# A decoder layer on one core: 512-column projection passes, and attention weights by differences of the values

## The chip, the cores and the metric

One core of one Trainium2 chip runs one launch of the kernel. The metric is the device time of the launch in microseconds. The core has five engines, each with a queue of its own that it works through strictly in order: PE (TensorE, matmuls and transposes, results to PSUM), DVE (VectorE), ACT (ScalarE), POOL (GpSimd) and SP, which issues nearly all DMA transfers. Every time below comes from one profiled execution, unless it is called a median of runs.

## The reference

One layer (`DEPTH = 1`) over 1024 tokens of 1024 channels, all float32:

```python
h = rms_norm(x, norm1_g)
q, k, v, glu_a, glu_b = split(h @ w_in, 5)                 # 512 columns each
q, k = rms_norm per head (8 heads of 64), times q_norm_g, k_norm_g
# attention, strictly causal, no softmax:
#   beta[t,s] = sigmoid(q_t.k_s / 8), s < t
#   A[t,s]    = beta[t,s] * prod_{s<j<t} (1 - beta[t,j])
#   attn_t    = sum_{s<t} A[t,s] v_s
c = glu_a * sigmoid(glu_b)
c = silu(layer_norm(causal_depthwise_conv31(c)))
x = x + concat([attn, c]) @ w_out
h = rms_norm(x, norm2_g)
g, u = split(h @ w_up, 2)                                   # 2816 columns each
x = x + (silu(causal_depthwise_conv3(g)) * u) @ w_down
```

## The kernel before

**Arithmetic.** Each float32 operand of a matmul is split into a high part (`hi`, an ACT cast to float32r) and a low part (`lo`, what is left, a subtraction on DVE or POOL), and a product is three matmuls, hi·hi, hi·lo and lo·hi (`mm3`, L313 to L315).

**Stages.** In the first stage the eight token tiles of x (128 tokens each) are loaded, squared (L419 on ACT), scaled by their norm (`rs` on POOL, L304 and L305; the scaling L423 on DVE), transposed on PE (`hT`, L432) and split (`h_hi` L436, `h_lo` L437). Then come the projections, in this order on PE: v of heads 0 to 3 (`v0`, its second half behind glu 0), the four gated channel blocks `glu` 0 to 3 of the convolution branch, then k, q of heads 0 to 3 and v of heads 4 to 7 (`k0`, `q0`, `v1`), each of these a pass of 256 columns (`project`, 8 tiles x 8 blocks of 128 channels x 3 matmuls of 128x256), and at last q and k of heads 4 to 7 together (`qk`, 512 columns). Weights come in as `raw`, and become `hi` (L459, ACT) and `lo` (L463, DVE or POOL). `normalized` scales q and k by head: a copy from PSUM (L478), then on ACT eight squares (L483) and eight scalings (L488) of 64 columns.

The convolution runs beside the projections: per channel block 31 taps in sequence on DVE (L615 to L627), 16 terms on ACT (L641) added up on POOL (L644), three closing subtractions (L657 to L659). When all four blocks are closed, `conv_norm` does the layer norm: transposes `ln` (L680), statistics on DVE, transposes `lnT` (L706), gate, product and split, and a store to DRAM.

Attention goes by heads and by tiles of 128 queries (`z{head}_{tile}`). For a query tile with w = 128 to 1024 keys: scores z on PE (L1084, L1085), two sigmoids on ACT, of -z into `nb` (`below`, L1094) and of z into `wt` (`above`, L1097), a running product from the diagonal backwards over `nb` on DVE (`scan`, L1113), and `wt` times the product of the keys behind it on POOL (`times`, L1116). The weights are transposed on PE (`wT`, L1137), split into `th` (a copy, L1146 or L1148, on ACT or DVE) and `tl` (DVE, L1153 or L1158), and multiplied with the split values (`po`, L1165). Between these, PE does the rest of `qk` and the convolution's half of the output projection (`op`).

After attention a second plan adds the attention half of the output projection (`opa`), norms the tokens and prepares the feed-forward part; `u` and `dn` (L1764), the feed-forward matmuls, fill the rest.

**What sets the order.** The first two parts are planned: `add(cost, emit, key, after, takes)` enters an operation with its engine and cost in ns (or several engines to choose from), a key (the time it should come at; `T(us)` turns microseconds of the first stage into keys), what it must follow, and the buffers it takes (`plan.token`). `Plan.run` simulates the engines with these costs and emits the operations in the order that comes out; `in_order` then fixes that order on PE, DVE, ACT and POOL. So the costs and keys decide the order on every engine, and what a wait does on the chip is decided there: an engine waits at its next instruction, and all behind it wait too. A buffer is a numbered slot: `nb` (4, also the pads of the convolution), `wt` (5: two raw-weight slots and three convolution outputs `co`), `whl` (8, split weights), `z` (2 PSUM banks), `s` and `o` (3 each).

## Time and profile before

| | |
|---|---|
| median of 3 runs | 1130.48 us (1130.3 to 1130.74) |
| the profiled execution | 1130.67 us, span 1128.9 us |
| busy, share of the span | PE 98%, DVE 79%, ACT 57%, POOL 54% |
| first stage, up to the first `ln` transpose | 203.6 us |
| attention, first score to last `po` | about 238 to 436 us |
| feed-forward | from about 500 us to the end |

A row of the profile names the line, the engine, the operation and its operands (out<-in), how often it came, its busy time, the mean duration of one, and how long the engine had been idle just before, with what ended that. Rows of DMA issues say when a transfer was asked for. The spans of consecutive matmuls overlap: a 128x512 one lasts 0.39 us in the rows, but the next one starts 0.23 us after it. So a busy PE is not yet a PE at its peak, and what one more matmul costs is read from the starts.

### The profile page before, as it was taken

To read this page: it belongs to the slowest core of one execution; us is meant where nothing else is said; L and a number is where in the kernel's file an instruction comes from. 1 tells how busy PE (TensorE), PEld (TensorE's weight loads), DVE (VectorE), ACT (ScalarE), POOL (GpSimd) and SP (SyncE) were. 2 spreads that over 40 slices of the span, in tenths; PEclk is the share of its full clock that TensorE was granted. 3 is DMA by queue.
4 is the path that set the end of the run, shared out by engine and by line. 5 is a ranking of instruction groups with operands and counts; after the bars stand their busy time and mean duration, and the time that the engine had idled before them with its cause. 6 is when DMAs were issued, how large, how long until landed. Compare 5 with 4: busy or idle time off the path is not lost.

```text
span 1128.9 us, 15893 instructions
## 1 busy us (share of the span) xinstructions
PE 1103.1 (98%) x5639; PEld 931.1 (82%) x5639; DVE 889.3 (79%) x1184; ACT 642.7 (57%) x1293; POOL 608.0 (54%) x519
## 2 busy tenths in 40 slices
PE   7999999999899998999999999999999999999998
PEld 6888899878788886878888888888888888888887
DVE  6399967579998987789887776777776678787795
ACT  6256699587877784663343333333343478776660
POOL 5077848387676752656342233233223189888670
PEclk8999999999999999999999999999999999999999
DMA  8021101223833304442232222222222392303404
GB/s 281 22 57 38 57 20 53 74 99 104 248 106 94 103 39 168 157 148 69 96 110 93 75 93 75 93 75 75 94 80 89 112 353 76 129 24 146 150 1 149
DMA packets 108636, 116.48 MB, mean 103 GB/s; under 512 B 20782, under 2 KB 88590, under 8 KB 108558
## 3 DMA queue, kind: packets, MB, share of 16 engines
q1 hardware_dynamic: 108414, 114.95, 30.9%
q8 instruction: 44, 0.72, 0.3%
q10 hardware_dynamic: 144, 0.52, 0.1%
q14 instruction: 34, 0.28, 0.1%
HBM read 82.95 MB, written 28.31 MB: 99 GB/s over the span
## 4 chain that ended last, share of the span: by engine, by line
PE 90%; DVE 4%; ACT 2%; DMA 2%; issue 1%; POOL 1%; SPq 0%; DVEq 0%; ACTq 0%; POOLq 0%
PE dn L1764 19%; PE u_S L314 7%; PE u_S L315 7%; PE u_S L313 7%; PE u L315 5%; PE u L313 5%; PE u L314 5%; PE po L1165 3%; PE wT L1137 2%; PE v L313 1%; PE v L314 1%; PE v L315 1%; PE glu_b L314 1%; PE glu_a L314 1%; PE glu_b L313 1%; PE glu_a L315 1%
## 5 line engine op out<-in xcount | busy, mean ns | idle before, releaser
L1764 PE MATMUL dn<-wd,wd 128*128 128x512 f32 x768 | 181.4, 389 | 0.0
L1764 PEld LDWEIGHTS dn<-wd,wd 128*128 128x128 f32 x768 | 144.2, 188 | 29.9
L314 PE MATMUL u_S<-bT,aS 128*128 128x512 f32 x264 | 102.8, 389 | 0.8 <-DVE bT L1439 0.8
L1767 DVE TENSOR_TENSOR c<-dn,c 128x512 f32<-128x512 f32 x120 | 81.4, 685 | 27.3 <-PE dn L1764 26.7
L315 PE MATMUL u_S<-bT,aS 128*128 128x512 f32 x264 | 102.7, 389 | 0.0
L313 PE MATMUL u_S<-bT,aS 128*128 128x512 f32 x264 | 102.5, 389 | 0.0
L1116 POOL TENSOR_TENSOR wt<-wt,nb 128x128 f32<-128x128 f32 (+3 forms) x64 | 78.0, 1224 | 42.8 <-DVE nb L1113 29.0
L309 ACT CAST aS<-rawu 128x512 fp32r<-128x512 f32 x63 | 38.9, 621 | 97.4 <-PE u_S L315 63.0
L1669 ACT CAST wd<-rawd 128x512 fp32r<-128x512 f32 x128 | 72.6, 618 | 31.3 <-DMA rawd<-in_w_down_dram 7.7
L1113 DVE TENSOR_TENSOR_SCAN nb<-nb,one 128x128 f32<-128x128 f32 (+3 forms) x64 | 84.7, 1340 | 3.1 <-ACT nb L1094 2.8
L1511 POOL TENSOR_TENSOR s<-rawu 128x512 f32<-128x512 f32 x21 | 29.4, 1400 | 103.6 <-DMA rawu<-in_w_up_dram 97.7
L1668 ACT COPY whole<-rawd 128x512 f32<-128x512 f32 x110 | 63.4, 585 | 25.8 <-DVE wd L1670 12.9
L1517 POOL TENSOR_TENSOR rawu<-rawu 128x512 f32<-128x512 f32 x21 | 29.9, 1426 | 80.7 <-DVE a L310 80.7
L1670 DVE TENSOR_TENSOR wd<-whole,wd 128x512 fp32r<-128x512 f32 x90 | 59.8, 683 | 13.0 <-ACT wd L1669 6.9
L1613 DVE SCALAR_TENSOR_TENSOR y<-gv,cols_a,y 128x1023 f32<-128x1023 f32 (+1 forms) x44 | 60.9, 1384 | 10.2 <-ACT y L1611 10.2
L309 ACT CAST a<-rawu 128x512 fp32r<-128x512 f32 x63 | 39.0, 621 | 50.0 <-PE u_S L315 30.2
L315 PE MATMUL u<-b,a 128*128 128x512 f32 x168 | 65.5, 390 | 0.0
L313 PE MATMUL u<-b,a 128*128 128x512 f32 x168 | 65.5, 390 | 0.0
L314 PE MATMUL u<-b,a 128*128 128x512 f32 x168 | 65.4, 389 | 0.0
L314 PEld LDWEIGHTS u_S<-bT,aS 128*128 128x128 f32 x264 | 49.6, 188 | 11.5 <-POOL raws L1476 1.2
L310 DVE TENSOR_TENSOR aS<-rawu,aS 128x512 fp32r<-128x512 f32 x63 | 53.3, 846 | 6.6 <-ACT aS L309 6.0
L313 PEld LDWEIGHTS u_S<-bT,aS 128*128 128x128 f32 x264 | 49.5, 188 | 10.5 <-ACT bT L1438 0.4
(362 smaller groups left out, 3435.2 us busy)
## 6 DMA issues: line engine op xcount, KB each, us to landing
rawu<-in_w_up_dram SPq DMA_DIRECT2D x44, 512.0 KB
act_d<-y SPq DMA_DIRECT2D x22, 512.0 KB
rawd<-act_d SPq DMA_DIRECT2D x22, 512.0 KB
rawd<-in_w_down_dram SPq DMA_DIRECT2D x22, 512.0 KB
rawo<-in_w_out_dram SPq DMA_DIRECT2D x8, 512.0 KB
m<-conv_d SPq DMA_DIRECT2D x16, 256.0 KB
xt<-in_x_dram SPq DMA_DIRECT2D x8, 512.0 KB
x_part<-xt SPq DMA_DIRECT2D x8, 512.0 KB
```

Source lines behind the costliest of these rows:

```text
L309: nc.scalar.copy(hi, src)
L313: nc.tensor.matmul(ps, a_hi, b_hi, start=first, stop=False)
L314: nc.tensor.matmul(ps, a_hi, b_lo, start=False, stop=False)
L315: nc.tensor.matmul(ps, a_lo, b_hi, start=False, stop=last)
L1113: nc.vector.tensor_tensor_scan(rev, rev, ones_of[0][:, :w], 0.0, op0=ALU.mult, op1=ALU.add)
L1116: nc.gpsimd.tensor_tensor(d["wt"][:, :w], d["wt"][:, :w], d["nb"][:, o + 1:S + 1], op=ALU.mult)
L1613: nc.vector.scalar_tensor_tensor(y[:, j:], g[:, :S - j], par("fw", (KF - 1 - j) * NF + f), y[:, j:], op0=ALU.mult, op1=ALU.add)
L1668: nc.scalar.copy(whole, src)
L1669: nc.scalar.copy(t[:, 0], src)
L1670: lo_engine.tensor_tensor(t[:, 1], whole, f32(t[:, 0]), op=ALU.subtract)
L1764: nc.tensor.matmul(ps, a[:, tok], b, start=first and m == 0, stop=last and m == 2, skip_group_check=True)
L1767: nc.vector.tensor_tensor(sums[c][s], ps, sums[c][s], op=ALU.add)
```

## The change

Three things change, with the order that follows from them.

**Projection passes.** `project` now makes 512 columns in a pass: v of all eight heads (`v`, written to the tiles `v0` and `v1`; two token tiles before glu 0, two behind it, four behind glu 1), and q and k of heads 0 to 3 together (`qk0`), before `qk`. The weights of a pass come in four pieces of 2 channel blocks x 512 columns (two DMAs each). The split weights of glu 0 and 1 and of one piece of `qk0` go to the pads and the `co` buffers. q and k of heads 0 to 3 are scaled by `summed` for all eight tiles, as tiles 6 and 7 of `qk` were before: one wide square on ACT, a `tensor_reduce` and a scaling (two of 256 columns) on DVE.

**The first tile.** The key of the first token tiles is earlier (`5 * t - 2` instead of `2 + 2 * t`), so that x's first tile is scaled ahead of the first split of a weight.

**Attention by parts.** With C(s) the running product from s up to the query, A[t,s] = C(s+1) - C(s), so the sum over A times v equals the sum over C(s) - 1 times (v of s-1, minus v of s). The sigmoid of z and the product with it are gone; `less` takes one from the running product, on POOL or ACT; the scan keeps the masked part at one (`max` with a corner of ones instead of `add` with a diagonal). The values are replaced by their differences once (`differences`): a shift by one token is a DMA from SBUF to SBUF, in 112 and 15 rows and one row across the tiles, then a subtraction of 128x1024 on POOL, two for each half of the heads. The weights stay in the buffer of the scan, which is now one of seven (four `nb`, three `co`).

```diff
-AHEAD_Z, AHEAD_SCAN = 1.7, 0.9
+AHEAD_Z, AHEAD_SCAN = 1.4, 0.5
+SUMMED_FIRST = (0, 1, 2, 3, 4, 5, 6, 7)
...
+    corner = const([P, P], BF16, "corner")
+    nc.gpsimd.affine_select(corner, zero_b, pattern=[[1, P]], base=-P, channel_multiplier=1, compare_op=ALU.is_ge, fill=1.0)
...
+    def differences(blk, key, after, tokens):
+        d = {}
+        def shift():
+            v = qkv["v", blk]
...
+            nc.gpsimd.memset(d["s"][0][0:1, 0, :], 0.0)
+            for n in range(2):
+                for r in (slice(0, 112), slice(112, P - 1)):
+                    nc.sync.dma_start(d["s"][n][r.start + 1:r.stop + 1], v[r, 4 * n:4 * n + 4, :])
+                nc.sync.dma_start(d["s"][n][0:1, 1 - n:4, :], v[P - 1:P, 3 * n:3 + 4 * n, :])
+        x = add("SP", 5000, shift, key, after, tokens)
...
+                (nc.gpsimd if eng == "POOL" else nc.vector).tensor_tensor(v, d["s"][n], v, op=ALU.subtract)
+            subs.append(add({"POOL": 2560}, sub, key, [x]))
...
+    def project(name, parts, ws, t, at_, room):
+        o, d, m = plan.token("o"), {}, None
+        tok = slice((t % 4) * P, (t % 4 + 1) * P)
+        for k in range(ND):
+            def products(k=k):
+                if k == 0:
+                    d["ps"] = bank(o, [P, 512], f"{name}{t}")
+                    room()
+                hi, lo = [ws[k // 2][part].rearrange("p k b c -> p k (b c)") for part in ("hi", "lo")]
+                mm3(d["ps"], h_hi[t // 4][:, k, tok], h_lo[t // 4][:, k, tok], hi[:, k % 2, :], lo[:, k % 2, :], k == 0, k == ND - 1)
...
-        norm_in(t, xl[t], (2 + 2 * t) if t < 4 else (8 + 3 * t))
-    project("v", 0, v0, (0, 1), (12, 18))
+        norm_in(t, xl[t], (5 * t - 2) if t < 4 else (8 + 3 * t))
...
-    for part, blk, at_, pairs in (("k", 0, 124, (0, 1, 2, 3)), ("q", 0, 147, (0, 1, 2, 3)), ("v", 1, 170, (2, 3, 0, 1))):
-        project(part, blk, project_weights(part, blk, at_), pairs, [at_ + 5.8 * i for i in range(4)])
+    done["q", 0] = done["k", 0] = [project("qk0_", (("q", 0), ("k", 0)), w_first, t, FIRST_QK + 5.5 * t, qk_room) for t in range(NT)]
...
-                    def above(d=d, n=n, cs=cs, ce=ce):
-                        nc.scalar.activation(d["wt"][:, cs:ce], d["z", n][:, :ce - cs], AF.Sigmoid)
...
-                    nc.vector.tensor_tensor_scan(rev, rev, ones_of[0][:, :w], 0.0, op0=ALU.mult, op1=ALU.add)
-
-                def times(d=d, o=o, w=w):
-                    nc.gpsimd.tensor_tensor(d["wt"][:, :w], d["wt"][:, :w], d["nb"][:, o + 1:S + 1], op=ALU.mult)
+                    nc.vector.tensor_tensor_scan(rev, rev, ones_of[0][:, :w], 0.0, op0=ALU.mult, op1=ALU.max)
+
+                def less(eng, d=d, o=o):
+                    nb = d["nb"][:, o:S]
+                    if eng == "POOL":
+                        nc.gpsimd.tensor_scalar(nb, nb, 1.0, -1.0, op0=ALU.mult, op1=ALU.add)
+                    else:
+                        nc.scalar.activation(nb, nb, AF.Identity, bias=minus_one)
...
-                b = add("POOL", 310 + 1.5 * w, times, i - AHEAD_SCAN + 0.3 * u, [a] + twos)
+                b = add({"POOL": 100 + 1.03 * w, "ACT": 160 + 0.86 * w}, less, i - AHEAD_SCAN + 0.3 * u, [a])
```

The order on the engines is built from both kernels. On DVE, at the very start (x_q0 and x_k0 hold the first two tiles of x, raw/hi/lo_v are the first weights), the rows are before:

```order
L463 TENSOR_TENSOR lo_v0_0_211<-raw_v0_0_194,hi_v0_0_210 128x1024
L423 SCALAR_TENSOR_TENSOR x_q0_133<-x_q0_133,rs0_207,attn_110 128x1024
L463 TENSOR_TENSOR lo_v0_1_218<-raw_v0_1_196,hi_v0_1_217 128x1024
L423 SCALAR_TENSOR_TENSOR x_q0_133<-x_q0_133,rs1_225,attn_110 128x1024
L437 TENSOR_TENSOR h_lo0_170<-hT0_0_227,h_hi0_169 128x4x128
L437 TENSOR_TENSOR h_lo0_170<-hT0_1_249,h_hi0_169 128x4x128
```

and after the change:

```order
L435 SCALAR_TENSOR_TENSOR x_k0_138<-x_k0_138,rs0_217,attn_110 128x1024
L483 TENSOR_TENSOR lo_v_0_223<-raw_v_0_200,hi_v_0_222 128x1024
L483 TENSOR_TENSOR lo_v_1_228<-raw_v_1_203,hi_v_1_227 128x1024
L449 TENSOR_TENSOR h_lo0_176<-hT0_0_231,h_hi0_175 128x4x128
L449 TENSOR_TENSOR h_lo0_176<-hT0_1_240,h_hi0_175 128x4x128
L435 SCALAR_TENSOR_TENSOR x_k0_138<-x_k0_138,rs1_238,attn_110 128x1024
L483 TENSOR_TENSOR lo_v_2_254<-raw_v_2_207,hi_v_2_253 128x1024
```

The scaling of the first tile has moved ahead of the first weight, and the second tile behind the split of the first.

On DVE, at the end of the last convolution block (conv_a3 and conv_b3 are its two sums), the rows are before:

```order
L627 SCALAR_TENSOR_TENSOR conv_b3_1776<-cpad3_916,cols_b_125,conv_b3_1776 128x512 x7
L527 COPY v1_1880<-v1_2_1881 128x512
L627 SCALAR_TENSOR_TENSOR conv_b3_1776<-cpad3_916,cols_b_125,conv_b3_1776 128x512
L527 COPY v1_1880<-v1_3_1959 128x512
L463 TENSOR_TENSOR lo_qk_0_2104<-raw_qk_0_1877,hi_qk_0_2103 128x1024
L463 TENSOR_TENSOR lo_qk_1_2120<-raw_qk_1_1895,hi_qk_1_2119 128x1024
L657 TENSOR_TENSOR attn_110<-attn_110,conv_a3_1601 128x512
```

and after:

```order
L704 SCALAR_TENSOR_TENSOR conv_b3_1570<-cpad3_1128,cols_b_129,conv_b3_1570 128x512 x2
L577 TENSOR_REDUCE sq_qk0_5_1646<-squares_qk0_5_1648 128x8
L704 SCALAR_TENSOR_TENSOR conv_b3_1570<-cpad3_1128,cols_b_129,conv_b3_1570 128x512 x4
L573 TENSOR_TENSOR q0_1343<-q0_1343,rs_qk0_5_1647 128x256
L573 TENSOR_TENSOR k0_1344<-k0_1344,rs_qk0_5_1647 128x256
L734 TENSOR_TENSOR attn_110<-attn_110,conv_a3_1416 128x512
L577 TENSOR_REDUCE sq_qk0_6_1692<-squares_qk0_6_1694 128x8
```

The reductions and scalings of `qk0` (tiles 0 to 6) now stand between the taps of the last block; `rs_qk0` in them is made on POOL, between the convolution's additions there.

On ACT, in attention, at head 3's query tile 6 (896 keys, two PSUM banks z), before:

```order
L1094 ACTIVATE nb0_0_2591<-z3_6_0_3611 128x512
L1097 ACTIVATE wt3_6_3617<-z3_6_0_3611 128x512
L1094 ACTIVATE nb0_0_2591<-z3_6_1_3614 128x384
L1097 ACTIVATE wt3_6_3617<-z3_6_1_3614 128x384
L1193 COPY attn_110<-po3_0_3571 64x512
```

and after, to the row that takes one from the running product of the same tile:

```order
L1176 ACTIVATE nb1_1_2396<-z3_6_0_3098 128x512
L1176 ACTIVATE nb1_1_2396<-z3_6_1_3102 128x384
L1197 ACTIVATE nb3_5_3085<-nb3_5_3085,minus_one_131 128x768
L1346 COPY prod1_1_3134<-op1_1_3036 128x512
L1226 CAST diagonal_0_1722<-wT3_0_0_3130 128x384
L1228 CAST rest_2108<-wT3_1_0_3136 128x512
L1176 ACTIVATE nb3_7_3152<-z3_7_0_3112 128x512
L1197 ACTIVATE nb1_1_2396<-nb1_1_2396,minus_one_131 128x896
```

The second sigmoid of each bank has gone; 30 of the 64 `less` stand on ACT, 34 on POOL, and 14 copies L1015, L1146 and L1148 have moved from DVE to ACT (29 on DVE before, 15 now).

More of the change, by code (lines that the diff above doesn't have):

```diff
@@ L443, with in_pad, in_co, weights @@
     norm_done = []
-    def weights(name, srcs, shape, at_, key=None):
+    def in_pad(r, shape, name):
+        return cp.tile([P, KC - 1 + S], F32R, tag=f"pad{r.index}", name=name)[:, :S].rearrange("p (k c) -> p k c", k=shape[0]) if len(shape) == 2 else (
+            cp.tile([P, KC - 1 + S], F32R, tag=f"pad{r.index}", name=name)[:, :S].rearrange("p (k b c) -> p k b c", k=shape[0], b=shape[1]))
+    def in_co(r, shape, name):
+        return wide(r, [P] + shape, name, F32R)
+    def weights(name, srcs, shape, at_, key=None, homes=None):
         d, room = {}, plan.token("wt")
-        room.only = (2, 3) if name.startswith("glu") and key is not None else (0, 1)
-        d["rooms"] = [plan.token("whl") for _ in range(2)]
+        room.only = (2, 3) if name in ("v_2", "v_3") else (0, 1)
+        homes = homes or [(plan.token("whl"), lambda r, shape, name: whl([P] + shape, F32R, name, r.index)) for _ in range(2)]
+        d["rooms"] = [r for r, _ in homes]
         def load():
@@ L457, in high @@
         def high():
-            d["hi"], d["lo"] = [whl([P] + shape, F32R, f"{part}_{name}", r.index) for part, r in zip(("hi", "lo"), d["rooms"])]
+            d["hi"], d["lo"] = [home(r, shape, f"{part}_{name}") for part, (r, home) in zip(("hi", "lo"), homes)]
             nc.scalar.copy(d["hi"], d["raw"])
@@ new lines, in summed, with groups, square, scale @@
+    def summed(name, d, o, m, to, at_):
+        room, r, key = plan.token("squares"), plan.token("rs8"), T(at_)
+        def groups(of):
+            return of.rearrange("p (h d) -> p h d", d=DH)
+        def square():
+            d["sq"], d["rs"] = [small.tile([P, 8], F32, tag=f"{tag}8_{r.index}", name=f"{tag}_{name}") for tag in ("sq", "rs")]
+            d["squares"] = squares(room, f"squares_{name}")
+            for n, piece in enumerate(to()):
+                nc.scalar.activation(part_of(d["squares"], n, 512 // len(to())), piece, AF.Square)
+        def scale():
+            for n, piece in enumerate(to()):
+                g = 8 // len(to())
+                nc.vector.tensor_tensor(groups(piece), groups(piece), d["rs"][:, n * g:(n + 1) * g].unsqueeze(2).to_broadcast([P, g, DH]), op=ALU.mult)
+        m = add({"ACT": 600, "DVE": 690}, lambda eng: copy_out(eng, to(), d["ps"]), key, [m])
+        a = add("ACT", 620, square, key, [m], [room, r])
+        b = add("DVE", 690, lambda: nc.vector.tensor_reduce(d["sq"], groups(d["squares"]), axis=AX.X, op=ALU.add), key, [a])
+        c = add("POOL", 1900, lambda: rstd(d["rs"], d["sq"], 1.0 / DH), key, [b])
+        e = add("DVE", 750, scale, key, [c])
+        room.users += [b]
+        r.users += [e]
+        o.users += [m]
+        return e
@@ new lines, in project, with to @@
+    def project(name, parts, ws, t, at_, room):
[8 more added lines that the diff above has]
+                mm3(d["ps"], h_hi[t // 4][:, k, tok], h_lo[t // 4][:, k, tok], hi[:, k % 2, :], lo[:, k % 2, :], k == 0, k == ND - 1)
+            m = add("PE", 685, products, T(at_ + 0.7 * k), [ws[k // 2]["ready"], h_ready[t][k // 4]] + ([m] if m else [] if name == "v" else list(norm_done)), [] if m else [o])
+            for r in ws[k // 2]["rooms"]:
+                r.users += [m]
+        if t > 3:
+            second_used.append(m)
+        def to():
+            return [qkv[part][:, t, :] for part in parts]
+        if name != "v":
+            return (summed if t in SUMMED_FIRST else normalized)(f"{name}{t}", d, o, m, to, at_ + 6)
+        a = add({"ACT": 700, "DVE": 800}, lambda eng: copy_out(eng, to(), d["ps"]), T(at_ + 6), [m])
+        o.users += [a]
+        return a
@@ L843, in to @@
             return qkv["both"][:, t, :]
[L845 to L866 removed]
+        qk_done[t] = (summed if t in SUMMED else normalized)(f"qk{t}", d, o, m, lambda: [to()], at_ + 6)
     for t in range(4, NT):
@@ L871 @@
         conv_norm(n, LN_AT + 10 * n)
+    rooms = [plan.token("wt", free=True) for _ in range(2)]
+    for n, r in enumerate(rooms):
+        r.only = (n,)
+    differences(1, DIFF_AT, done["v", 1] + second_used, rooms)
     def make_one():
@@ L934 @@
         queries_keys(t)
-    early, late = {}, {}
+    early, late, n_tile = {}, {}, [0]
     base = 0.0
```

167 lines of the change are left out of this document (79 added, 88 removed).

## The prediction

> **What bounds the kernel now.** I read the page's shares and chain first, then the stages, then the waits of the stage in which PE stands.
>
> ```profile
> span 1128.9 us, 15893 instructions
> PE 1103.1 (98%) x5639; PEld 931.1 (82%) x5639; DVE 889.3 (79%) x1184; ACT 642.7 (57%) x1293; POOL 608.0 (54%) x519
> PE 90%; DVE 4%; ACT 2%; DMA 2%; issue 1%; POOL 1%; SPq 0%; DVEq 0%; ACTq 0%; POOLq 0%
> ```
>
> The profiled execution took 1130.67 us, 1.8 outside its span and 0.2 over the median. PE carries the chain. By stages (first column of each engine: busy us):
>
> ```profile
> 0.00:20.00 20.00, 13.73 (x60) 9.18 (x61) 10.89 (x14) 13.12 (x21) 9.23 (x17) 0.83 0.95 320
> 20.00:203.00 183.00, 183.00 (x1183) 167.49 (x1183) 141.08 (x187) 117.14 (x317) 110.65 (x95) 1.00 0.18 53
> 203.00:238.00 35.00, 34.91 (x190) 28.84 (x188) 22.11 (x37) 23.18 (x71) 19.54 (x29) 1.00 0.18 66
> 238.00:436.00 198.00, 187.56 (x1183) 161.76 (x1182) 182.34 (x225) 156.08 (x333) 137.11 (x123) 0.99 0.38 114
> 436.00:520.00 84.00, 78.91 (x364) 63.05 (x363) 66.80 (x96) 45.12 (x87) 45.73 (x47) 0.98 0.45 150
> ```
>
> From 20 to 238 us PE never rests: there time is only had by giving PE less to do. In attention (238 to 436) PE is idle for 10.4 us, and DVE is busy for 182.3 of 198. So the start, the passes and attention are three different questions.
>
> **1. Passes of 512 columns.** PE loses 768 matmuls of 256 columns (v, k and q: 2 x 2 x 8 tiles x 8 blocks x 3) and gets 384 of 512. Their starts:
>
> ```profile
> 19.24 0.28 PE L314 MATMUL v<-lo_v,h_hi 128*128 128x256 f32 x1
> ...
> 20.20 0.28 PE L313 MATMUL v<-hi_v,h_hi 128*128 128x256 f32 x1
> ...
> 99.81 0.39 PE L313 MATMUL glu_b<-h_hi,hi_glu_b 128*128 128x512 f32 x1
> ...
> 100.72 0.39 PE L314 MATMUL glu_b<-h_lo,hi_glu_b 128*128 128x512 f32 x1
> ```
>
> Eight starts of 256 columns take 0.96 us, 0.120 each; four of 512 take 0.91, 0.2275 each. 768 x 0.120 - 384 x 0.2275 = 92.2 - 87.4 = 4.8 us less, all of it where PE never rests. By rounding of the starts (0.01 us) the bounds are 3.5 to 6. [...]
>
> The wider passes need 24 loads of 256 KB on SP instead of 8 of 512 and 8 of 256 KB; in 20 to 203 the transfers fill 18% of the queues, and that covers them. If it were gone, a late piece would stop PE at its first matmul: the split weights of v stay in all eight `whl` slots until v's last tile, so those of glu 2 are made only behind the last use of a piece, with 18 matmuls (4.1 us) of cover for a cast (1.04 us, below) and a split (1.22). glu 3's load waits on SP behind the shift of the values, that is for v's last tile, and has the 21.8 us of glu 2 (96 x 0.2275) as cover. I take 0, at worst 1 us.
>
> **2. The start.**
>
> ```profile
> 7.71 0.56 POOL L305 TENSOR_TENSOR rs<-rs,expo 128x1 f32<-128x1 f32 x1
> 7.80 1.04 ACT L459 CAST hi_v<-raw_v 128x1024 fp32r<-128x1024 f32 x1 [0.46 <-DMA raw_v<-in_w_in_dram]
> 8.88 1.23 DVE L463 TENSOR_TENSOR lo_v<-raw_v,hi_v 128x1024 fp32r<-128x1024 f32 x1 [7.20 <-ACT hi_v L459]
> 10.02 1.28 DVE L423 SCALAR_TENSOR_TENSOR x_q<-x_q,rs,attn 128x1024 f32<-128x1024 f32 x1
> 10.57 1.06 ACT L419 ACTIVATE attn_first<-x_q 128x1024 f32<-128x1024 f32 x1 [0.23 <-DMA x_q<-in_x_dram]
> 11.36 1.97 PE L432 MATMUL hT<-ident_r,x_q 128*128 128x128 f32 x8 [3.39 <-DVE x_q L423]
> 14.60 1.94 PE L432 MATMUL hT<-ident_r,x_q 128*128 128x128 f32 x8 [1.27 <-DVE x_q L423]
> 16.55 0.41 PE L314 MATMUL v<-lo_v,h_hi 128*128 128x256 f32 x1
> 16.76 0.41 PE L315 MATMUL v<-hi_v,h_lo 128*128 128x256 f32 x1
> ```
>
> `rs` is there at 8.27, the scaling waits behind `lo_v` until 10.02. Put first, it runs 8.3 to 9.6, and `hT` 9.6 to 11.6. The first `h_hi` on ACT follows the square of the second tile (10.57 to 11.8, its load still the fourth of SP): 12.4. So v begins at 12.4, where before PE ran without a break from 14.6: 2.2 us. Against it, the cast, scaling and split of pieces 3 and 4 run between, about 1.2 us each on DVE; by 17.4 all four are split, and PE then still has half of the first v tile. At the start the clock is half (starts 0.21 us apart at 256 columns, 0.120 at 19.24), and if it rises at the same moment as before, only 0.8 of the 2.2 is left. I take 1.8, bounds 0.5 and 2.6. Ten transfers (v's other half among them) now stand before glu 0's; PE has 11 us of v for them, 16 x 0.5 MB at the 320 GB/s of the first row end by 27 us and glu 0 starts at about 29: cover enough, just.
>
> **3. The last convolution block.**
>
> ```profile
> L617 DVE SCALAR_TENSOR_TENSOR conv_a<-cpad,cols_b,conv_a 128x512 f32<-128x512 f32 x60 | 45.3, 755 | 2.0
> L659 DVE TENSOR_TENSOR conv_out<-attn,conv_b x4: 672/678/680, 86.8 to 198.5; 128x512 f32<-128x512 f32 x4
> L680 PE MATMUL ln<-ident_r,conv_out x32: 270/272/273, 203.6 to 231.0; 128*128 128x128 f32 x32
> L862 DVE TENSOR_TENSOR qk<-qk,rs_qk x2: 1007/1258/1508, 239.6 to 256.0; 128x512 f32<-128x512 f32 x2
> L920 DVE TENSOR_TENSOR qk<-qk,rs_qk x8: 399/415/415, 235.4 to 290.8; 128x256 f32<-128x256 f32 x8
> L860 DVE TENSOR_REDUCE sq_qk<-squares 128x8 f32<-128x512 f32 x1 | 0.7, 678 | 0.0
> ```
>
> Before, block 3 closes at 199.2 and `ln` starts at 203.6: 4.4 us to spare. After, PE ends glu 3 at about 151 (13.3 us of start, then 7 of `hT`, 43.7 of v, 87.4 of glu) and `qk0` at 195; three `ln` follow at once, in front of `qk`. DVE ends block 2 at about 157 (it starts at 130 behind glu 2), and block 3 then takes 31 taps (0.675 from start to start), three closings (0.6), six reductions (0.6) and twelve scalings (0.34 each, the 415 of L920 less the same 0.08): 30.3 us, 187. The scalings wait for `rs` on POOL, behind the convolution's additions there, some 0.4 us each time: 190. With both operands in SBUF they may also wait for POOL itself: L862 took 1007 and 1508, where twice L920 (which reads PSUM) is 830. Six tiles x 0.2 to 0.7 are 1 to 4 us: 191 to 194, just in time. PE stands 0 to 5 us; I take 1. [...]
>
> **4. Attention.**
>
> ```profile
> L1113 DVE TENSOR_TENSOR_SCAN nb<-nb,one 128x128 f32<-128x128 f32 (+3 forms) x64 | 84.7, 1340 | 3.1 <-ACT nb L1094 2.8
> L1116 POOL TENSOR_TENSOR wt<-wt,nb 128x128 f32<-128x128 f32 (+3 forms) x64 | 78.0, 1224 | 42.8 <-DVE nb L1113 29.0 <-PE qk L314 4.0 <-PE z L1085 2.5
> L1097 ACT ACTIVATE wt<-z 128x512 f32<-128x512 f32 (+2 forms) x96 | 47.9, 501 | 0.3
> L1148 DVE CAST rest<-wT 128x512 fp32r<-128x512 f32 x9 | 6.1, 681 | 0.4 <-PE po L1165 0.4
> L1146 DVE CAST diagonal<-wT 128x384 fp32r<-128x384 f32 x13 | 7.0, 540 | 0.9 <-PE wT L1137 0.8
> L1015 DVE CAST keys<-kT 128x512 fp32r<-128x512 f32 x7 | 4.7, 681 | 0.4 <-PE kT L1011 0.4
> L994 POOL TENSOR_SCALAR rest<-v x6: 621/628/630, 255.0 to 392.2; 128x512 fp32r<-128x512 f32 x6
> L1222 ACT CAST w_hh<-rawo 128x1024 fp32r<-128x1024 f32 x4 | 4.1, 1072 | 0.0
> DVE tl L1158 <- ACT rest L1148: 4.1, 7, 1.0
> DVE nb L1113 <- ACT nb L1094: 2.8, 6, 0.8
> DVE diagonal L1153 <- ACT diagonal L1146: 1.7, 2, 1.6
> DVE rest L1052 <- ACT keys L1049: 1.4, 2, 1.2
> DVE attn L1196 <- ACT attn L1193: 1.0, 3, 0.4
> ```
>
> DVE is the engine nearest its end, and 11.0 of its 15.7 idle us are waits for ACT (the last five rows). ACT loses 47.9 and gets 30 `less` (650 keys on average; between 0.7, a copy's rate by L1222, and 0.9 with its added column) = 21 to 27, and 14 copies = 7.8: 156 becomes 137 to 143. POOL loses 78.0 and gets 34 `less` (512 keys on average, the same operation as L994, 0.63) = 21 and two subtractions of 2.0: 137 becomes 84. DVE loses 3 x 0.68 + 6 x 0.54 + 5 x 0.68 = 8.7; rows overlap by 0.08, and one split of the convolution comes over from POOL: 6.5 net. The scan with `max` I take as the scan with `add`; no row shows another. One chain gets shorter too, since a large tile waits 2.0 us for `times` now and 1.1 for `less`, and its two z banks for one sigmoid each instead of two.
>
> So DVE's 182.3 become 176, and of its idle 15.7 I take a quarter off, as ACT's load falls by a tenth and the rest are chains: 176 + 12 = 188, 10 us less. Bounds: the whole idle gone would be 22 us, but PE's own starts (288 x 0.11, 320 x 0.12, 192 of z, 192 + 68 x 0.2275 and 124 x 0.11) fill 175 of the 198 already, so 20; at the other end, work off DVE gains nothing if the chains hold, and 30 new waits of ACT for a scan cost: a loss of 6. The shift of the values (1 MB per half of the heads) and its subtractions lie 100 us before their use: 0.
>
> **5. Behind attention** the order is the same, but the last split of w_out stands before the last sum of attention instead of behind it: 0.5 us less, bounds 0 and 1.2.
>
> **Sum:** 1130.7 - 4.8 - 1.8 + 1 - 10 - 0.5 = 1114.6, and by the median's 0.2, 1114.4.
>
> **The rivals.** (a) Attention is held by its chains: the order on every engine is fixed by costs in ns, and PE and DVE already alternate. For it: DVE's second cause of idleness is its own late work. Attention gains 4 and the whole ends at 1120.4. [...] (c) Slower: the 30 `less` on ACT wait for a scan, up to 2.27 us long, and behind them on ACT stand sigmoids and copies on which PE and DVE wait. Before, nothing on ACT waited for DVE's scan. The forecast's 16 us are eaten when each costs 0.54 us on the path; at 0.7 the time is 1135. Against it: `less` stands behind other rows in ACT's order, which cover a scan. (d) Everything in attention falls to PE's own 175 plus 5: 1106.5. (e) The pass saves no time because the weight load bounds it: 1119; the 0.120 and 0.2275 speak against it.
>
> **Chances.** Forecast (1109 to 1118) 0.6, (a) 0.17, (b) 0.08, (c) 0.05, (d) 0.06, (e) 0.04. 1106 to 1122 leaves out (c), part of (a) and of (d). 0.2% is what a measurement of this kernel tells from no change; faster has all cases but (c) and a remainder: 0.93, same 0.02, slower 0.05.
>
> **What the profile after would show.** Right: v's first matmul by 12.4; no idle PE between 20 and 195; `ln` at 195 to 197; the first z at 231 to 234, the last `po` at 420 to 424; DVE's waits for ACT under 8 us. Wrong: PE idle before `ln` with block 3 as releaser; ACT rows released by the scan, with PE waiting for them.

## The result, and the profile after

The changed kernel takes 1132.91 us (median of 12 runs, 1132.33 to 1136.43) against 1130.07 for the kernel before on the same chip (12 runs): the ratio is 1.0028, with a 95% interval of 1.0019 to 1.0037. It is slower by 2.8 us, where 1114.4 was forecast. The profiled execution took 1132.88 us, with this page:

```profile
span 1130.7 us, 14860 instructions
PE 1102.3 (97%) x5255; PEld 909.7 (80%) x5255; DVE 901.8 (80%) x1197; ACT 606.9 (54%) x1083; POOL 552.1 (49%) x487
```

ACT and POOL have 36 and 56 us less to do, PE has 384 matmuls less, and yet PE is busy for as long as before (1103.1) and the span is longer by 1.8. To see where, both spans are cut at the same events: the end of the projections of the first heads (the first `qk` of heads 4 to 7 before, the first `ln` after), the first `z`, the first product with w_out that belongs to attention (`opa`), the first `u` of the feed-forward part, and its first `dn`. The stages of before, then of after (columns: the stretch, its length, busy us of PE, PEld, DVE, ACT, POOL with instructions, the granted clock, share and GB/s of DMA):

```profile
0.00:201.56 201.56, 195.29 (x1234) 175.49 (x1235) 150.90 (x200) 129.51 (x336) 119.88 (x111) 0.98 0.26 79
201.56:238.23 36.67, 36.58 (x197) 30.22 (x196) 23.18 (x38) 24.16 (x74) 19.77 (x29) 1.00 0.18 66
238.23:436.31 198.08, 187.64 (x1184) 161.75 (x1182) 182.65 (x225) 156.10 (x333) 136.88 (x123) 0.99 0.38 115
436.31:493.38 57.07, 53.07 (x249) 42.67 (x248) 41.61 (x67) 30.79 (x62) 28.84 (x34) 0.97 0.51 179
493.38:915.38 422.00, 420.91 (x1856) 347.69 (x1857) 320.99 (x389) 166.82 (x244) 147.85 (x104) 1.00 0.30 97
```

```profile
0.00:197.69 197.69, 192.56 (x851) 155.16 (x852) 161.81 (x209) 97.87 (x167) 107.55 (x103) 0.98 0.26 79
197.69:243.66 45.97, 39.19 (x205) 32.35 (x203) 32.15 (x57) 29.46 (x84) 27.90 (x37) 0.93 0.33 105
243.66:437.15 193.49, 183.00 (x1178) 158.55 (x1175) 176.21 (x215) 147.60 (x279) 85.43 (x91) 1.00 0.39 121
437.15:490.38 53.23, 51.29 (x250) 41.47 (x248) 39.70 (x64) 29.92 (x61) 28.54 (x34) 1.00 0.52 178
490.38:917.30 426.92, 426.59 (x1857) 348.95 (x1858) 322.94 (x389) 166.42 (x244) 148.32 (x104) 1.00 0.29 96
```

Row by row: -3.9, +9.3, -4.6, -3.8 and +4.9, +1.9 together; behind `dn` it is -0.1, which makes the 1.8 by which the spans differ. Two rows eat what the other three gain, and each is a story of its own.

**The second row** holds the waits of PE that were forecast as 1 us. The timeline of PE, its waits, and DVE's last subtraction of a convolution block (L736) and its scalings (L573, with least, median and greatest ns):

```profile
197.69 0.49 PE L757 MATMUL ln<-ident_r,conv_out 128*128 128x128 f32 x3
204.59 2.15 PE L757 MATMUL ln<-ident_r,conv_out 128*128 128x128 f32 x9 [6.42 <-ACT q L528]
206.40 0.78 PE L325 MATMUL qk<-hi_qk,h_hi 128*128 128x512 f32 x1
L736 DVE TENSOR_TENSOR conv_out<-attn,conv_b x4: 677/678/679, 84.6 to 203.8; 128x512 f32<-128x512 f32 x4
L573 DVE TENSOR_TENSOR q<-q,rs_qk x8: 417/481/1306, 164.3 to 211.5; 128x256 f32<-128x256 f32 x8
L573 DVE TENSOR_TENSOR k<-k,rs_qk x8: 418/1412/2622, 165.5 to 211.9; 128x256 f32<-128x256 f32 x8
```

PE turns three of the four conv blocks of the first `ln` and stops at the fourth. The row names ACT's copy; what also had to be there is block 3, and its last subtraction started at 203.8 and took 0.68 us, up to 0.1 us before PE goes on. The matmul behind then takes 0.78 us in place of 0.39: the granted clock was 0.74 in the pause (197.8 to 204.5) and 0.51 from 204.6 to 207.9 (0.93 over the second row). Of the 9.3 us, 6.7 are PE's idle time (45.97 less 39.19, where it was 0.1), 0.9 are eight more transposes in the row, and the other 1.7 are slower starts, nearly all of them right behind the pause.

**The fifth row** is code that the change does not touch, with the same matmuls, and PE does not wait for more in it (idle for 0.3 us, 1.1 before). PE simply runs slower there, in `u` almost alone. The first and last `u` of one block of 36 and the first `u_S` behind it, after:

```profile
625.80 0.39 PE L325 MATMUL u<-bT,a 128*128 128x512 f32 x1
...
633.93 0.39 PE L327 MATMUL u<-b,a 128*128 128x512 f32 x1
634.16 0.39 PE L325 MATMUL u_S<-bT,aS 128*128 128x512 f32 x1
```

8.36 us for 36 matmuls, 0.2322 each, where before each took 0.2267 (8.16). The `u_S` between take 10.89 per 48, as before.

### The profile page after: what moved, and what is told of

The parts are those of the page before. It is cut to its first block, busy times and chain, and to the rows that moved or that the text cites. A ratio compares the mean times of both kernels' runs of the same rounds, so it can differ in the third digit from the quotient of the medians.

```text
span 1130.7 us, 14860 instructions
## 1 busy us (share of the span) xinstructions
PE 1102.3 (97%) x5255; PEld 909.7 (80%) x5255; DVE 901.8 (80%) x1197; ACT 606.9 (54%) x1083; POOL 552.1 (49%) x487
## 4 chain that ended last, share of the span: by engine, by line
PE 78%; DVE 11%; POOL 3%; ACT 3%; DMA 2%; issue 1%; SPq 0%; POOLq 0%; DVEq 0%; ACTq 0%
PE dn L1844 19%; PE u_S L326 7%; PE u_S L327 7%; PE u_S L325 7%; PE u L326 6%; PE u L325 5%; PE u L327 5%; PE po L1245 2%; POOL attn L721 2%; DVE conv_a L694 2%; PE wT L1217 2%; DVE nb L1190 2%; DVE conv_b L704 1%; PE opa L325 1%; PE opa L326 1%
## 5 line engine op out<-in xcount | busy, mean ns | idle before, releaser
L1190 DVE TENSOR_TENSOR_SCAN nb<-nb,one 128x128 f32<-128x128 f32 (+4 forms) x64 | 84.7, 1341 | 1.6 <-ACT nb L1176 1.4
L322 DVE TENSOR_TENSOR a<-rawu,a 128x512 fp32r<-128x512 f32 x63 | 50.2, 797 | 16.1 <-ACT a L321 16.1
L1593 POOL TENSOR_TENSOR rawu<-s,rawu 128x512 f32<-128x512 f32 x21 | 32.2, 1536 | 53.0 <-DVE a L322 52.2
```

Of the source, the lines that this page charges most:

```text
L322: lo_engine.tensor_tensor(lo, src, f32(hi), op=ALU.subtract)
L1190: nc.vector.tensor_tensor_scan(rev, rev, ones_of[0][:, :w], 0.0, op0=ALU.mult, op1=ALU.max)
```

## Experiments on the unchanged code: where the weights lie

All tiles have the same shape, and the order is the same; what differs is where they lie. The new constants (`corner`, `minus_one` and the longer set of small tiles) move everything allocated behind them in the left pools by 416 bytes. Both kernels also allocate a constant `pad` of 32 bytes that nothing reads, which makes the left pools easy to move.

```diff
 after_moved32, before_moved32:
-    const([P, 8], F32, "pad")
 after_moved96:
-    const([P, 8], F32, "pad")
+    const([P, 32], F32, "pad")
 before_right32:
+    ctx.enter_context(tc.tile_pool(name="edge", bufs=1, side="right")).tile([P, 8], F32, ...)
```

> The changed kernel with the unused 32-byte constant `pad` left out, and nothing else: the order on every engine is the same, but the left pools of SBUF (mixp and what lies behind it) move down by 32 bytes, so that their tiles start at odd multiples of 32 bytes, as in the kernel before, and no longer at multiples of 64. Theory A (the address of the weight tile sets PE's pitch): in the trace of the changed kernel matmuls of 512 columns whose weights start at a multiple of 64 bytes take 233.3 ns from start to start, all others 226.67; here all take 226.67, 36 `u` take 8.16 us in place of 8.36, the stretch from the first `u` to the first `dn` falls from 426.9 to 422, glu 0 and glu 1 fall by 1 us, and the whole by 5 to 6 us: about 1127. Rival B (the unchanged part is slower because other work or code loading falls on it at another moment): the same 426.9, the whole within 1 us of 1132.9.

> The kernel before with the same unused 32-byte constant left out, and nothing else: its left pools move down by 32 bytes, from odd multiples of 32 to multiples of 64. Theory A: the weights `a` of `u`, which lie there, now cost 233.3 ns per matmul in place of 226.67; the stretch from the first `u` to the first `dn` grows from 422.0 by 4 to 5 us, and the whole to 1134.5 to 1136. Rival B: no change, 1130.1 within 1.

> The changed kernel with the unused constant `pad` 128 bytes long in place of 32, same order on every engine: the left pools move up by 96 bytes. The runs so far leave of theory A this form: a matmul of 512 columns takes 226.67 ns where its weights and its moving operand start at the same place modulo 512 bytes, and 232 to 234 where they do not. (Before: all at 480 modulo 512. Changed kernel: weights `a` of `u` at 384. The two kernels moved by 32 bytes have them at 352 and 448: both slow, though 352 and 480 agree modulo 128.) Here `a` is at 480 again: 36 `u` take 8.16 us in place of 8.36, the stretch from the first `u` to the first `dn` about 422 in place of 426.9, and the whole 4 to 5 us less than the changed kernel: 1128 to 1129. Rival B (the place does not matter; something else in the new order slows `u`): 426.9 again, 1132.9.

> The kernel before with 32 unused bytes at the far end of SBUF, so that the right pools (the activations `b` and `bT`, the weights `aS`, `wd`) move down by 32 bytes to 448 modulo 512, while the left pools (weights `a`) stay at 480. Theory A, relative form (weights against moving operand): `u` with `a` on the left against `b` on the right is slow, 8.35 us per 36, while `u_S` and `dn`, with both on the right, stay at 226.67 ns: the whole 4 to 6 us over the kernel before. Rival A2 (absolute form: whatever starts elsewhere than at 480 is slow): `u_S` and `dn`, over 2000 matmuls, are slow as well, 10 to 20 us over. Rival B: no change.

The stretch from the first `u` to the first `dn`, in the order after_moved32, before_moved32, before_right32, after_moved96:

```profile
491.94:918.01 426.07, 425.75 (x1856) 349.32 (x1857) 321.07 (x389) 166.33 (x244) 147.81 (x103) 1.00 0.29 96
491.76:917.16 425.40, 424.31 (x1857) 347.43 (x1857) 321.46 (x389) 166.87 (x244) 148.66 (x104) 1.00 0.30 96
491.39:916.94 425.55, 424.47 (x1856) 347.69 (x1857) 321.74 (x389) 166.67 (x244) 147.66 (x104) 1.00 0.30 96
489.37:911.73 422.36, 421.94 (x1856) 348.79 (x1857) 321.56 (x389) 166.17 (x244) 147.02 (x103) 1.00 0.29 97
```

With the byte at which the tiles start, as the compiled program has it (the first of the three `a` in the left pools, which serve two thirds of `u`; the other two lie multiples of 4096 further), and the ratio of times to the kernel before:

```
kernel           a on the left mod 512  b, bT, aS mod 512   u to dn   ratio [95%]
before           56800        480       480                 422.00    1
changed          57216        384       480                 426.92    1.0028 [1.0019, 1.0037]
after_moved32    57184        352       480                 426.07    1.0015 [1.0005, 1.0026]
before_moved32   56768        448       480                 425.40    1.0038 [1.0025, 1.0051]
before_right32   56800        480       448                 425.55    1.0028 [1.0017, 1.0039]
after_moved96    57312        480       480                 422.36    0.9984 [0.9975, 0.9994]
```

My first form of the theory (a multiple of 64 bytes is slow) fell with after_moved32: 352 is an odd multiple of 32, like 480, and was slow. The form that these rows allow is relative: a 512-column matmul runs at 226.7 ns when its 128x128 weights and its moving operand start at the same place modulo 512 bytes, and at 232.9 to 233.2 on average when they do not (the 540 starts of `u` per kernel with `a` on the left). before_right32 shows that it is relative and not one good address: there `b`, `bT` and `aS` all moved to 448, and `u_S` (both on the right) kept its 10.89 us per 48, while `u` (`a` on the left still at 480) rose to 8.32 per 36.

In the changed kernel the weights of glu 0 and 1, in the convolution's padded tiles (4216 bytes long, so that the next one starts elsewhere) and in `conv_out`'s, show the same: 5.55 to 5.60 us per 24 where 5.44 was seen before. They also show that 512 is too strict, though the expectations above and below are worded with it. The tile `hi_glu_a` of glu 0 starts at 224 modulo 512 in the changed kernel and in after_moved96 alike, against activations at 480; the tile `lo_glu_a`, whose matmuls stand between, starts at 384 in the first and at 480 in the second. The first, then the second:

```profile
41.01 0.39 PE L325 MATMUL glu_a<-h_hi,hi_glu_a 128*128 128x512 f32 x1
...
43.80 0.40 PE L325 MATMUL glu_b<-h_hi,hi_glu_b 128*128 128x512 f32 x1
...
49.37 0.39 PE L325 MATMUL glu_a<-h_hi,hi_glu_a 128*128 128x512 f32 x1
...
52.09 0.39 PE L325 MATMUL glu_a<-h_hi,hi_glu_a 128*128 128x512 f32 x1
```

Twelve starts lie between the two rows of each kernel, and take 2.79 us in the first and 2.72 in the second; those of `hi_glu_a` alone average 233 and 227 ns. So 224 against 480, 256 bytes apart, is fast when its neighbours are, and slow beside a slow one. What the rows bear out is a step of 256 bytes: distances of 0 and 256 were fast; 32, 128, 384, 416 and 480 were slow. Other distances do not occur in these kernels, and why the distance matters no run shows.

No wait of PE is recorded for this (in the fifth row it is idle for 0.3 us), but the same matmuls take nearly 3% longer (233 ns for 226.7) when the two operands lie badly to each other.

## Experiments on the last convolution block

Theory: DVE's scalings, new before 200 us, are drawn out by POOL's additions, as the forecast allowed for in its third part, and close block 3 late. DVE's and POOL's rows at one of them show what is meant:

```profile
185.56 1.09 POOL L721 TENSOR_TENSOR attn<-attn,attn_first 128x512 f32<-128x512 f32 x1
186.38 0.54 DVE L573 TENSOR_TENSOR q<-q,rs_qk 128x256 f32<-128x256 f32 x1
186.72 1.36 POOL L721 TENSOR_TENSOR attn<-attn 128x512 f32<-128x512 f32 x1
186.85 1.52 DVE L573 TENSOR_TENSOR k<-k,rs_qk 128x256 f32<-128x256 f32 x1
...
193.45 2.59 POOL L483 TENSOR_TENSOR lo_qk<-raw_qk,hi_qk 128x1024 fp32r<-128x1024 f32 x1
193.70 2.62 DVE L573 TENSOR_TENSOR k<-k,rs_qk 128x256 f32<-128x256 f32 x1
```

Of the twelve scalings that start before 204, nine are drawn out, and each of them ends 0.27 to 0.29 us behind an instruction of POOL: eight behind an addition, and the longest behind the split of a weight. Alone a scaling takes 0.42.

**Read from PSUM.** The copy out of PSUM goes, square and scaling read the bank:

```diff
-            for n, piece in enumerate(to()):
-                nc.scalar.activation(part_of(d["squares"], ...), piece, AF.Square)
+            nc.scalar.activation(d["squares"], d["ps"], AF.Square)
...
-                nc.vector.tensor_tensor(groups(piece), groups(piece), d["rs"]...)
+                nc.vector.tensor_tensor(groups(piece), groups(part_of(d["ps"], n, 512 // len(to()))), d["rs"]...)
...
-        m = add({"ACT": 600, "DVE": 690}, lambda eng: copy_out(eng, to(), d["ps"]), key, [m])
...
-        o.users += [m]
+        o.users += [a, e]
```

> The changed kernel with the norms of the first heads' queries and keys (and of two tiles of the others) read from PSUM: ACT no longer copies the product out, its square and DVE's scaling read the bank, and the scaling writes the tile in SBUF. In the changed kernel's trace the 16 scalings of 256 columns, whose two operands lie in SBUF, take 418 ns where POOL runs no two-operand addition and 1.2 to 2.6 us where it does, each ending 0.2 to 0.3 us behind POOL's. Theory E (two operands from SBUF wait for POOL; one does not): all take about 0.4 us, DVE has 8 to 9 us less to do before 195, `ln` waits under 1 us, and the whole falls by 6 to 8 us, to 1125 to 1127. Rival F (the scalings were slow for another reason, the broadcast operand): they stay at 0.7 to 1.5 us, and the whole stays within 2 us of 1132.9.

```profile
L572 DVE TENSOR_TENSOR q<-qk,rs_qk x8: 415/417/419, 164.1 to 203.1; 128x256 f32<-128x256 f32 x8
L572 DVE TENSOR_TENSOR k<-qk,rs_qk x8: 411/414/415, 164.4 to 203.4; 128x256 f32<-128x256 f32 x8
```

Measured: 1129.27 us, ratio 0.9991 [0.9982, 0.9999]. All sixteen scalings take 0.41 to 0.42 us, though POOL's additions run beside ten of them; theory E holds, and with it the wait at `ln` is gone (0.4 us is left). The time fell by 3.6 us only (the expectation was 6 to 8), and not where it was looked for: from the first `ln` to z it still takes 46.3 us (46.0 after the change), and attention is 3.6 shorter. The order was worked out anew, more work now stands ahead of z, and PE waits further on:

```profile
PE lnT L781 <- DVE attn L763: 3.7, 2, 2.9
```

**Four scalings by a factor per partition,** in the same order:

```diff
-                nc.vector.tensor_tensor(groups(piece), groups(piece), d["rs"]... , op=ALU.mult)
+                for i, group in enumerate(...):
+                    nc.vector.tensor_scalar(group, group, d["rs"][:, n * g + i:n * g + i + 1], None, op0=ALU.mult)
```

> The changed kernel with each scaling of 256 columns (two operands from SBUF, one of them the factors, broadcast) written as four scalings of 64 columns by a per-partition factor, which leaves one operand in SBUF; the order on every engine is otherwise the same. Theory E (two operands from SBUF wait for POOL's two-operand addition): no scaling is drawn out to the end of an addition; each group of four takes 0.5 to 0.8 us whatever POOL does, against a mean of 0.75 (`q`) and 1.48 (`k`) in 150 to 205; DVE has 3 to 7 us less, PE's wait at `ln` of 6.4 us falls to 0 to 3, the whole by 3 to 7 us: 1126 to 1130. Rival F (the third block is late for its taps and reductions alone): the wait stays at 6.

```profile
L574 DVE TENSOR_SCALAR q<-q,rs_qk x28: 241/249/2333, 164.7 to 213.0; 128x64 f32<-128x64 f32 x28
L574 DVE TENSOR_SCALAR k<-k,rs_qk x28: 239/244/1093, 167.2 to 213.7; 128x64 f32<-128x64 f32 x28
PE ln L758 <- ACT squares_qk L568: 13.0, 1, 13.0
```

1141.2 us, ratio 1.0095 [1.0082, 1.0108]: a miss. A single scaling takes 0.24 us when nothing holds it, but 13 of 40 are drawn out, to the end of POOL's instruction: up to 1.3 us by an addition, and to 2.3 by the split of a weight. So it is not the second operand from SBUF alone: DVE's `tensor_scalar` from SBUF to SBUF waits as well, while the taps (L694, one operand in SBUF, the sum in PSUM) take 756 ns beside the same additions. Why it waits no run here shows.

**`ln` later in the order** (key 199 in place of 190, 33 `qk` ahead of it), and **the norms on ACT** as before the change:

```diff
 after_ln199:
-LN_AT = 190.0
+LN_AT = 199.0
 after_norm_on_act:
-SUMMED_FIRST = (0, 1, 2, 3, 4, 5, 6, 7)
+SUMMED_FIRST = ()
```

> The changed kernel with the key of the convolution's norm at 199 in place of 190: on PE 33 matmuls of `qk` (7.5 us) now stand ahead of the first `ln`, which is where the changed kernel's PE stood for 6.4 us and then ran 2.3 us longer at half clock. Theory C (`ln` was put ahead of work that was ready, and the late third block of the convolution stops PE): no wait at `ln` over 1 us, clock full throughout, z begins at about 237 in place of 243.7, and the whole falls by 5 to 8 us, to 1125 to 1128. Rival D (attention's first tiles are held by DVE, which is late for the same reason): z comes earlier, but PE stands as long between z and the first sums, and the whole stays within 2 us of 1132.9.

> The changed kernel with the norms of the first queries and keys done on ACT as before the change (eight squares with accumulation and eight scalings of 64 columns per tile; the order is worked out anew). DVE loses eight reductions (0.68 each) and sixteen scalings (mean 0.94 in 150 to 230), about 20 us up to the last; ACT gets 64 squares (0.255 and 0.187 for the accumulator) and 64 scalings (0.334) for 16 squares: 43 us more, where it is busy for 23 of 45 us between 150 and 195. Theory K (DVE's new work before 200 made the third block late): `ln` waits under 1 us, and PE reaches the `qk` behind it 7 us earlier. Rival L (ACT then holds PE's banks or the weights' casts): PE waits for ACT between 155 and 200, and the whole is 1130 or more.

```profile
PE qk L325 <- ACT hi_qk L479: 3.7, 1, 3.7
ACT hi_qk L479 <- DMA raw_qk<-in_w_in_dram: 4.6, 1, 4.6
```

after_ln199 took 1142.61 us, ratio 1.0105 [1.0092, 1.0118]. `ln` waits no more, but the `qk` put ahead of it was not ready: its weights come late (the rows above, of that run), and z begins at 247.0. So `ln` did not stand in front of ready work, as theory C had it; two things were late at once. The later z is 3.4 us of the loss, and attention behind it, in another order, is 7.0 us longer. after_norm_on_act took 1144.08, ratio 1.0115 [1.0101, 1.0129]: `ln` does not wait either (theory K), but PE waits 3.0 us for ACT's cast of the next weights (rival L), and attention, in another order, takes 206.7 us.

## Experiments on attention

Theory G: the 30 `less` on ACT, which wait for DVE's scan, hold back what is behind them. The waits of the changed kernel speak for it:

```profile
ACT nb L1197 <- DVE nb L1190: 11.7, 17, 2.2
DVE tl L1238 <- ACT rest L1228: 6.3, 7, 2.0
DVE diagonal L1233 <- ACT diagonal L1226: 3.0, 5, 1.2
```

Three edits:

```diff
 after_less_on_pool:
-                b = add({"POOL": 100 + 1.03 * w, "ACT": 160 + 0.86 * w}, less, ...)
+                b = add({"POOL": 100 + 1.03 * w}, less, ...)
 after_no_less: nothing is taken from the running product; both instructions of less() become
+                        pass
 after_ahead_as_before:
-AHEAD_Z, AHEAD_SCAN = 1.4, 0.5
+AHEAD_Z, AHEAD_SCAN = 1.7, 0.9
```

> The changed kernel with all 64 `less` on POOL, none on ACT (the order in attention is worked out anew with it). In the changed kernel's trace ACT waits 11.7 us for DVE's scan at `less`, and DVE 14 us for ACT in attention. Theory G (ACT's `less` holds back the sigmoids and copies behind it): both shrink, ACT has 25 us less to do, and attention, 193.5 us from the first z to the first product with w_out, falls by 4 to 8 us; the whole 1125 to 1129. Rival H (attention is held by its chains and by DVE's own work of 176 us): attention falls by less than 2 us.

> The changed kernel with all 64 `less` left out (nothing is taken from the scanned values, so the attention weights are off by one and the output is not the reference's); the order of all other work is the same. ACT loses 25.2 us and POOL 22.5, and each tile's chain loses its last step of 0.3 to 1.1 us and a hand-over. Theory I (attention is held by the chain of each tile, scan to transposes): attention, 193.5 us from the first z to the first product with w_out, falls by 5 us or more, to 185 to 188. Rival J (PE and DVE, with 176 us each of their own work, and the fixed order of both hold it): it falls by less than 3 us, and DVE's waits for ACT (14 us) stay over 10.

> The changed kernel with z and the scan planned as far ahead as in the kernel before (1.7 and 0.9 steps in place of 1.4 and 0.5); the order in attention is worked out anew. Theory M (with the scan planned only half a step ahead the chain of a tile has too little lead, which is why DVE's idle time grew from 15.5 to 17.3 us although ACT and POOL were relieved): attention falls by 2 to 5 us, whole 1128 to 1131. Rival N (the chains were no tighter than before): within 1 us, or worse, since tiles hold their slots for longer.

Attention, from the first z to the first `opa`, in this order:

```profile
243.54:439.64 196.10, 184.24 (x1177) 159.25 (x1176) 176.42 (x214) 126.08 (x250) 107.43 (x119) 1.00 0.38 116
241.64:433.05 191.41, 182.17 (x1178) 158.58 (x1176) 174.84 (x215) 126.09 (x249) 64.53 (x57) 1.00 0.39 122
244.46:447.25 202.79, 189.13 (x1181) 160.67 (x1180) 179.20 (x217) 155.15 (x290) 77.14 (x78) 0.99 0.37 113
```

Theory G falls. Without any `less` on ACT attention is 2.6 us longer (whole: 1141.15, ratio 1.0088 [1.0075, 1.0101]; behind it PE waits 2.6 us for the split of w_out, and the granted clock is 0.94 up to `u`, where it is 1.00 after the change). Without any `less` at all, in the same order, it is 2.1 us shorter (1131.0, ratio 1.0007 [0.9998, 1.0016]): the waits of 11.7 us and 48 us of work on two engines are worth 2 us of time. DVE's busy time hardly moves in these two (174.8 to 176.4), and attention follows it with 17 to 20 us on top. Planned as far ahead as before, attention is 9.3 us longer (1145.4, ratio 1.013 [1.0116, 1.0144]), so the shorter lead was no loss. Rivals J and N hold: DVE's waits for ACT stay at 14 us without any `less`, and the order alone is worth more than all the work of `less`. That PE and DVE and the fixed order between them set the time is what is left; no run changed their order alone.

## Both remedies together, and what stays open

```diff
 psum_and_places: after_psum_scale, and
-    const([P, 8], F32, "pad")
+    const([P, 32], F32, "pad")
-    cp.tile([P, KC - 1 + S], ...)
+    cp.tile([P, 1152], ...)
```

> The changed kernel with both remedies: the norms of the first queries and keys read from PSUM (as in after_psum_scale), the unused constant of 128 bytes (as in after_moved96), and the four padded tiles 4608 bytes long in place of 4216, so that weights of glu 0, glu 1 and of the first queries and keys that lie in them start at 480 modulo 512 bytes too. Theories A and E together: glu 0 and 1 take 5.44 us per 24 matmuls in place of 5.55 to 5.60 (1 us less up to the first `qk`), `ln` does not wait, the stretch from the first `u` to the first `dn` takes 422, and the whole is that of after_psum_scale (1129.3) less 5 to 6: 1123 to 1124.5, which beats both kernels. Rival: if the place of the weights matters only to `u` and the gain of after_moved96 was partly something else, 1125 to 1127.

```profile
0.00:196.56 196.56, 191.54 (x851) 155.12 (x851) 160.86 (x221) 97.21 (x154) 110.89 (x107) 0.98 0.27 83
196.56:243.66 47.10, 42.76 (x215) 34.97 (x214) 27.80 (x46) 27.92 (x77) 29.73 (x37) 0.93 0.31 101
243.66:433.49 189.83, 181.84 (x1165) 157.07 (x1164) 170.67 (x209) 144.96 (x276) 82.71 (x88) 1.00 0.39 120
486.19:908.17 421.98, 420.91 (x1856) 347.68 (x1857) 318.32 (x389) 166.99 (x244) 146.93 (x104) 1.00 0.30 97
```

1123.72 us (1123.0 to 1124.45), ratio 0.9939 [0.9926, 0.9951]: faster than both kernels, by about what the two remedies and the padded tiles add up to. `u` is back at 8.16 us per 36, and the blocks of 24 of glu 0 and 1 are at 5.44. But the second row is no shorter than after the change. z still begins at 243.66; what the scalings no longer take came back in attention, where DVE has 5.5 us less to do. Two runs asked whether the order alone holds the second row:

```diff
 places_ln196:
-LN_AT = 190.0
+LN_AT = 196.0
 places_turns8, for lnT and what follows:
-            k = T(at_ + 5 + c)
+            k = T(at_ + 8 + c)
```

> psum_and_places with the key of the convolution's norm at 196 in place of 190: on PE the first `ln` stands behind 18 more `qk`, and the sixteen `lnT` of the second half, which stood in one piece, stand in pieces of four with `qk` between. Theory O (the order alone makes the wait of 3.9 us at `lnT` and the half clock behind it): no wait at `lnT` over 1 us, z begins at 237 to 240 in place of 243.7, and the whole falls by 3 to 6 us to 1118 to 1121. Rival P (DVE and POOL have too much to do before z): PE waits elsewhere before z, z begins at 242 or later, and the whole stays within 1.5 us of 1123.7 or is worse, as with the key at 199 in after_ln199, where the weights of the next `qk` came late.

> psum_and_places with the keys of the turning back (`lnT` and what follows it) three units later, the first `ln` unmoved. On PE `lnT` of the second half stand behind three more `qk` and as twelve and four in place of sixteen, and the first half's first `lnT` still follow `ln`. Theory O: the wait at `lnT` falls from 3.9 to 1 to 3 us, and the whole by 1 to 3 us. Rival P: same within 1 us, z at 243 or later.

```profile
PE qk L325 <- DVE qk L996: 5.1, 1, 5.1
PE ln L755 <- ACT conv_out L808: 4.3, 3, 2.7
PE lnT L781 <- DVE attn L763: 4.3, 2, 2.7
```

Both are slower than psum_and_places: 1132.83 (first two rows), ratio 1.0021 [1.0012, 1.003], with z at 249.6, and 1127.45 (last row), 0.997 [0.9957, 0.9983], with z at 243.8. Theory O gains nothing from either order; that no order would do better is not shown. The 47.1 us between the first `ln` and z, where before it was 34.6 (203.6 to 238.2), can be taken apart by the trace. PE starts 132 matmuls of `qk` and 81 transposes there, 117 and 69 before: at the usual 0.2267 and 0.108 us that is 4.7 us more work, which came forward and is no loss. PE waits for 4.3 us, most of it for DVE at `lnT`, and the other 3.5 are slower starts (the granted clock is 0.93). Why DVE is late at `lnT`, and whether an order without that wait exists, stays open.

## Why the prediction was wrong, step by step

By the rows, the result lies over the forecast by 8.3 us between the projections and z, 5.4 in attention, 4.9 behind w_out and 2.7 before the first `ln`, and under it by 3.3 behind attention: 18.0 of the 18.5 in all. The first is the largest: the third block of the convolution, priced at a wait of 1 us.

- **Passes and start** (forecast -4.8 and -1.8): together -3.9 up to the first `ln`, and -5.0 in psum_and_places. The 512-column starts cost what the rows said, but only where the weights lie well; the new homes of the weights of glu 0 and 1 took back some 0.9 us (the first `ln` is at 197.43 in after_psum_scale, and at 196.56 in psum_and_places, where those weights lie well). The step "weights in other rooms" had been priced at nothing. The start came true in its place (v's first matmul at 12.50, forecast 12.4), but PE ran these first matmuls at half clock (0.50 granted, 0.427 us from start to start, until 16.5). If the passes gave their 4.8, nothing to 0.2 us was left for the start, under its lower bound of 0.5; no run measures the two apart.
- **Block 3** (forecast +1, bounds 0 and 5): +9.3 in the row, 6.4 of it the wait. This is the step that failed most: the wait was named and priced too low. Two terms of its sum were mis-sized. The contention was put at 0.2 to 0.7 us for a tile, 1 to 4 in all; the twelve scalings that start before 204 took 13.4 us for 5.0 alone, 8.4 more. And the taps were put at 0.675 us from start to start. That is a tap in front of some other instruction; a tap in front of a tap, which takes up the sum that the first one wrote, takes 0.79, in the kernel before too:

```profile
158.33 9.46 DVE L617 SCALAR_TENSOR_TENSOR conv_a<-cpad,cols_b,conv_a 128x512 f32<-128x512 f32 x12
167.69 0.68 DVE L478 COPY q<-q 128x512 f32<-128x512 f32 x1
```

  So 31 taps took 23.9 us in block 2 and 22.9 in block 3, where 20.9 was reckoned. Block 2, which I let end at 157, began 2.3 us after its time (132.3) and closed at 164.2. Less the 8.4 us, block 3 would have closed at about 196, in time for PE, and in after_psum_scale it closes at 195.1; but there the whole gained 3.6 us and not 9. For the contention I had rows: L862 at 1007 and 1508 against 830. I averaged over them instead of asking what POOL does in that stage: its additions (L721) take 25.6 us between 150 and 195.
- **The half clock behind a pause** was left out: behind the 6.4 us of waiting, nine `ln` and three `qk` took 1.6 us longer than at their usual spacing (0.43 us and more from `qk` to `qk`, in place of 0.2267; the granted clock was 0.51 from 204.6 to 207.9), so that the wait cost some 8.
- **Attention** (forecast -10, rival (a) -4 at 0.17): -4.6. The sums of work came out for DVE and POOL (DVE -6.4 for a forecast of 6.5, POOL 85.4 for 84; ACT 147.6 for 137 to 143). What failed is "of its idle 15.7 I take a quarter off": idle DVE rose from 15.4 to 17.3. Relieving ACT did not shorten the chains: without any `less` DVE is still idle for 16.6 (after_no_less). Rival (a) had the size, and its reason is the one left standing.
- **Behind attention** (forecast -0.5): -3.8. Before, PE waited 1.07 us for the split of w_out, and twice for less, and ran at half clock from 440.6 to 444.2 (0.52 granted, 0.43 us from `opa` to `opa`); after, it did neither (1.00 granted in the row). In the row PE is idle for 2.1 us less and busy for 1.8 us less, so the clock was nearly half of it.
- **Everything behind w_out** (forecast 0, not even named): +4.9. Without it the sign would have been the one forecast: after_moved96, with nothing else mended, is faster than the kernel before, by 0.16%. The step that failed is the unspoken one, that code which is not edited keeps its time.

Rival (c), `less` behind a scan on ACT, has its waits in the trace (11.7 us) and next to no price: leaving out every `less` gained 2 us in attention, and moving them all off ACT lost 2.6.

## What to carry to other kernels

Before costing an edit at nothing elsewhere, look at what it allocates: a few constants moved every tile behind them, and a saturated PE lost 1.2% over 420 us with not one wait to show for it; the pitch of the same matmul before and after is the view that finds it. Where DVE work between SBUF tiles is moved into a stage in which POOL adds, price it at POOL's durations (1.1 to 2.6 us here) and not at its own (0.42), and read from PSUM where there is a choice (0.41 to 0.42 beside POOL's additions in after_psum_scale). The pitch of a tap here depended on what followed it (0.79 us or 0.66): read a pitch from a row like the one that is to be priced. A stall of PE cost its length here (6.4 us) and 1.6 us more at half clock behind it (0.51 granted), and work taken from an engine that only waits in turn with others was worth little (2.1 us for all of `less`).
